# The first MLP product by Strassen's algorithm, the second product's weights in groups of four row tiles by two column tiles

## The chip, the core and the metric

The kernel runs on one core of a Trainium2 chip. The metric is device time in microseconds (us), from the runs of the compiled program. The engines named below work from queues of their own: TensorE (PE) multiplies 128x128 weight tiles by 128x320 tiles of activations into PSUM, ScalarE (ACT) and VectorE (DVE) do elementwise work, SyncE (SP) issues the loads of the weights.

## The reference, cut to what matters

The reference is one inference step of a two-layer encoder (`DEPTH = 2`) over 640 tokens: 512 of a new stream and 8 times 16 of running streams. Attention, a convolution branch and a short gated convolution are merged and projected; the part that the change touches comes after that:

```python
x = layer_norm(DN_ALPHA * x + merged @ w_mix_out, ln1_g, ln1_b)
hdn = jnp.square(jax.nn.relu(x @ w_ff1 + b_ff1))                 # 1024 -> 4096
x = layer_norm(DN_ALPHA * x + (hdn @ w_ff2 + b_ff2), ln2_g, ln2_b)   # 4096 -> 1024
```

All of it is in float32.

## The kernel before

Activations lie with features on the partitions: 8 tiles of 128 features by 640 tokens, and the tokens are worked in two halves of 320 (`HF`). Each float32 value is cut into two float32r parts (h and l), and a product of two such pairs takes three matmuls, h·h, h·l and l·h (`mm3_steps`, L357, L359 and L361). So a 1024x4096 product is 8 x 32 weight tiles x 3 matmuls x 2 halves = 1536 matmuls, and a layer's MLP has two such products.

Weights come through `Stream`. A group is 8 tiles of 128x128: one DMA of 512 KB on SP's queue into one of two `raw` buffers; ACT copies it into `wh` (L192), DVE subtracts to get `wl` (L193). Groups of the product before a norm (`mix`, `ff2`) are centred first: ACT passes over the group once for the means of its rows (L187, L188), then cuts (L189, and L190 on DVE). The cut pair lives in one of nine buffers during the MLP.

What sets the order: each engine executes a list written at build time, in which the framework's scheduler has put the instructions by their priority in the program (`tc.high_priority` moves them up). An instruction that waits holds back all that follow it on its engine.

Around the change the program does this, per layer. The output projection (`mix`) of half 0, then of half 1. The residual `r` of each half takes up the product on DVE (L333), its squares are summed (ACT L336, DVE L338), a column sum on PE (`pvn`) and a chain of twelve tiny DVE operations (L388 to L395) give the reciprocal root, PE spreads it over the partitions (`rbn`), DVE scales the eight tiles of `r` (L426), ACT and DVE cut them into `xh` and `xl` (L1043, L1044), and ACT scales `r` once more for the second residual (L1046). While half 1 goes through this, PE works on the first eight column tiles of the first MLP product for half 0 alone, 8 x 24 = 192 matmuls. Then follow the same eight for half 1, and after that chunks of four column tiles (`ff1(c)`, results `mm_ff`, through relu, square and cut on ACT and DVE as `ft`, `fq`, `hh`, `hl`) alternate with the second product of the chunk before (`ff2(c)`, results `f`, added to `r` by DVE). The last two chunks are done half by half, so that half 0's second norm lies under half 1's matmuls.

Of the kernel before, what the change touches and what calls it, by code (L numbers as in the profile page):

```python
# [19 lines left out]
P = 128  # L20
# [24 lines left out]
LOOK = 7  # L45
WARM = 12
# [22 lines left out]
def beside(i):  # L69
    """What the tensor engine does beside step i of the prompt's attention: the next heads, the absorbed queries or the side branches."""  # L70
    if i < 0:
        return "ssssss"
    if 2 <= i % 8 < 5 and i < 24:
        return "hhh"
    return "aas" if 24 <= i < 32 else "sss"


def block_groups(l):
    """The dense weights of one layer in the order of their use: groups of (name, row tile, column tile)."""
# [42 lines left out]
    for c in range(2, 8):
        ff1(c)
        if c < 7:
            ff2(c - 1)
    ff2(6)
    ff2(7)
    return g


def plan():
    out, off = [], 0
    for l in range(DEPTH):
        for g in block_groups(l):
            out.append((l, tuple(g), off))
            off += len(g) * P * P
    return out, off


def slots(g):  # L140
    """The pool of weight buffers that each group of a layer goes to."""
    n = next(i for i, q in enumerate(g) if q[0][0] == "mix")
    late = list("AAbbBBBb")
    late += [("bAAbbBBBb")[i % 9] for i in range(len(g) - n - 16)]
    return ["b"] * n + late + list("bbbbABBB")


class Stream:
    """Weights, group by group: loaded ahead and cut exactly into two float32r parts.

    Groups of the products before a norm have the mean of their rows taken off, so that
    the products have mean zero over the features."""

    def __init__(self, tc, w_ap, groups, raw_pool, part_pool, hp=400):
# [5 lines left out]
        self.held = set()  # L160

# [11 lines left out]

    def _emit(self):
        i = self.done
        self.done += 1
        _, g, off = self.groups[i]
        n, c = len(g) * P, self.slot[i]
        pp, bufs = self.pools[c]
        with self.tc.high_priority(offset=self.hp):  # L180
            raw = self.rp.tile([P, GRP * P], F32, tag="raw", name=f"raw{i}")
            self.nc.sync.dma_start(raw[:, :n], self.w[off:off + P * n].rearrange("(p n) -> p n", p=P))
            wh = pp.tile([P, GRP * P], F32R, tag="wh", name=f"wh{i}")
            wl = pp.tile([P, GRP * P], F32R, tag="wl", name=f"wl{i}")
            if g[0][0] in ("mix", "ff2"):
                nm = self.rp.tile([P, 1], F32, tag="nm", name=f"nm{i}", bufs=4)
                self.nc.scalar.activation(out=raw, in_=raw, func=AF.Copy, accum_out=nm)  # L187
                self.nc.scalar.mul(out=nm, in_=nm, mul=-1.0 / D)  # L188
                self.nc.scalar.activation(out=wh, in_=raw, func=AF.Identity, bias=nm, scale=1.0)  # L189
                self.nc.vector.scalar_tensor_tensor(out=wl, in0=raw, scalar=nm, in1=R(wh), op0=ALU.add, op1=ALU.subtract)  # L190
            else:
                self.nc.scalar.activation(out=wh[:, :n], in_=raw[:, :n], func=AF.Copy)  # L192
                self.nc.vector.tensor_tensor(out=wl[:, :n], in0=raw[:, :n], in1=R(wh[:, :n]), op=ALU.subtract)  # L193
# [3 lines left out]
    def _can(self):  # L197
# [4 lines left out]
        if c not in self.pools:  # L202
            return False
# [3 lines left out]
    def _ahead(self):  # L207
        while self._can() and self.done < self.at + (LOOK if self.groups[self.done][1][0][0] in ("mix", "ff1", "ff2") else 2):
            self._emit()
# [5 lines left out]
    def next(self, l, *keys, hold=False):  # L215
        i = self.at
        self.at += 1
        ll, g, _ = self.groups[i]
        assert ll == l and all(k in g for k in keys), (i, l, keys, ll, g)
# [10 lines left out]
        blk.i = i  # L230
        return blk
# [10 lines left out]
def trunk(tc, A, O):  # L242
# [18 lines left out]
    def open_banks(tag, **tags):  # L261
        """The PSUM banks beside psT for one phase: a pool for each name, with so many buffers."""
# [7 lines left out]
        if "op" in tags:  # L270
            # one bank for the attention's outputs, kept from phase to phase
# [15 lines left out]
    # the tensor engine's clock rises with its first products: before the data is there  # L287
# [9 lines left out]
    def split(h, lo, src, scale=None):  # L297
        """h + lo == src, 12 significant bits each."""
# [25 lines left out]
    def mm_pair(name, hs=(0, 1), ps=None):  # L324
        """One bank for each half of the tokens; the pairs of banks take turns."""
# [5 lines left out]
    def add_r(i, m, o, r, ss=None, tmp=None, tag=""):  # L331
        """r += o; ss = the sum of the squares of the tiles of r"""
# [7 lines left out]
    def center(ri, s, tag):  # L340
        """ri <- ri - its mean over the features; s is the sum of its tiles"""
# [35 lines left out]
    def rsqrt_rows(ss, starts, scale, eps, tmp, tag):  # L377
        """rs[t, c] = 1/sqrt(scale * sum_p ss[p, starts[c] + t] + eps)"""
# [850 lines left out]
```

## Time and profile before

| | |
|---|---|
| device time, median of 3 runs (lowest to highest) | 2058.18 us (2058.05 to 2060.56) |
| span of the profiled execution | 2053.8 us |
| TensorE matmul busy | 2029.3 us, 99% of the span, 13600 instructions |
| TensorE weight load busy | 1956.7 us, 95% |
| VectorE busy | 1137.9 us, 55% |
| ScalarE busy | 881.0 us, 43% |
| mean of the granted TensorE clock | 0.994 of full speed |

The span runs from the first to the last instruction of the profiled execution; the 4.4 us by which the median of the runs is longer lie around it. Busy times overlap between engines. A matmul's own duration (0.31 us) is longer than the distance from its start to the next one's start, because successive matmuls overlap; the distance is what counts. Line numbers are those of the kernel before.

### The profile page before, as it was taken

Reading aid. Unit: us, or ns where it says so; the run is one execution under the profiler, and the core shown is the slowest. Engines: PE = TensorE matmul, PEld = TensorE weight load, DVE = VectorE, ACT = ScalarE, POOL = GpSimd, SP = SyncE. Lnnn points to the kernel's source line nnn. Section 1 sums busy time; section 2 is a strip of 40 time slices with the busy share of each in tenths; the row PEclk is TensorE's granted clock in tenths of the full one; section 3 lists DMA queues with packets and bytes.
Section 4 is the critical chain, followed back from the end, with each engine's and each line's share of the span. In section 5 each row is a group of like instructions: output and inputs, shape, how many; then the busy total and the mean of one; then the engine's idle time right before and its main releaser. Section 6 shows DMA issues by size and latency. Waiting matters only on the chain.

```text
span 2053.8 us, 33262 instructions
## 1 busy us (share of the span) xinstructions
PE 2029.3 (99%) x13600; PEld 1956.7 (95%) x13600; DVE 1137.9 (55%) x2476; ACT 881.0 (43%) x1734; POOL 21.8 (1%) x39
## 2 busy tenths in 40 slices
PE   9999999999999999999999989999999999999997
PEld 9887899999999999999998878999999999999997
DVE  5754469776565333333677545697766553333335
ACT  5564222245473434445356532223354734333352
POOL 0000000000000000000010000000000000000000
PEclk9999999999999999999999999999999999999999
DMA  6113322222222222222242034222233222222111
GB/s 197 50 39 99 111 78 75 78 67 88 85 91 85 65 78 62 83 72 73 64 138 64 24 107 105 80 83 64 73 98 93 84 82 73 72 62 72 63 62 52
DMA packets 56041, 163.83 MB, mean 80 GB/s; under 512 B 10033, under 2 KB 13537, under 8 KB 55889
## 3 DMA queue, kind: packets, MB, share of 16 engines
q1 hardware_dynamic: 54016, 156.55, 24.8%
q0 software_dynamic: 1872, 5.17, 1.0%
q8 instruction: 106, 1.74, 0.4%
q14 instruction: 47, 0.38, 0.1%
HBM read 157.01 MB, written 4.69 MB: 79 GB/s over the span
## 4 chain that ended last, share of the span: by engine, by line
PE 95%; DMA 2%; ACT 1%; DVE 1%; issue 0%; SPq 0%; ACTq 0%; DVEq 0%
PE mm_ff L359 7%; PE f L359 7%; PE mm_ff L357 7%; PE mm_ff L361 7%; PE f L361 7%; PE f L357 7%; PE mm_g L357 6%; PE mm_g L359 6%; PE mm_g L361 5%; PE op L733 2%; PE mix L361 2%; PE mix L357 2%; PE mix L359 2%; DMA raw<-in_W_dram 2%; PE ol L881 1%; PE tp L720 1%
## 5 line engine op out<-in xcount | busy, mean ns | idle before, releaser
L192 ACT ACTIVATE wh<-raw 128x1024 fp32r<-128x1024 f32 (+3 forms) x186 | 183.3, 986 | 329.6 <-PE mm_g L359 201.2
L193 DVE TENSOR_TENSOR wl<-raw,wh 128x1024 fp32r<-128x1024 f32 (+3 forms) x186 | 210.7, 1133 | 193.0 <-ACT wh L192 189.8
L359 PE MATMUL f<-hl,wh 128*128 128x320 f32 x1024 | 259.3, 309 | 0.0
L357 PE MATMUL f<-hh,wh 128*128 128x320 f32 x1024 | 258.6, 308 | 0.0
L361 PE MATMUL f<-hh,wl 128*128 128x320 f32 x1024 | 258.6, 308 | 0.0
L359 PE MATMUL mm_ff<-xl,wh 128*128 128x320 f32 x1024 | 253.9, 309 | 0.0
L357 PE MATMUL mm_ff<-xh,wh 128*128 128x320 f32 x1024 | 253.6, 308 | 0.0
L361 PE MATMUL mm_ff<-xh,wl 128*128 128x320 f32 x1024 | 253.3, 308 | 0.0
L333 DVE TENSOR_TENSOR r<-r,f 128x320 f32<-128x320 f32 x256 | 116.1, 483 | 188.1 <-PE f L361 187.8
L189 ACT ACTIVATE wh<-raw,nm 128x1024 fp32r<-128x1024 f32 x80 | 90.4, 1146 | 228.2 <-PE f L359 214.7
L190 DVE SCALAR_TENSOR_TENSOR wl<-raw,nm,wh 128x1024 fp32r<-128x1024 f32 x80 | 101.5, 1283 | 155.9 <-ACT wh L189 155.8
L357 PE MATMUL mm_g<-xh,wh 128*128 128x320 f32 x768 | 181.9, 311 | 0.0
L361 PE MATMUL mm_g<-xh,wl 128*128 128x320 f32 x768 | 181.0, 309 | 0.0
L359 PE MATMUL mm_g<-xl,wh 128*128 128x320 f32 x768 | 180.5, 309 | 0.0
L361 PEld LDWEIGHTS f<-hh,wl 128*128 128x128 f32 x1024 | 177.7, 188 | 0.2
L359 PEld LDWEIGHTS f<-hl,wh 128*128 128x128 f32 x1024 | 177.7, 188 | 0.2
L357 PEld LDWEIGHTS f<-hh,wh 128*128 128x128 f32 x1024 | 177.4, 188 | 0.3
L359 PEld LDWEIGHTS mm_ff<-xl,wh 128*128 128x128 f32 x1024 | 176.5, 188 | 0.0
L357 PEld LDWEIGHTS mm_ff<-xh,wh 128*128 128x128 f32 x1024 | 176.5, 188 | 0.0
L361 PEld LDWEIGHTS mm_ff<-xh,wl 128*128 128x128 f32 x1024 | 176.4, 188 | 0.0
L187 ACT ACTIVATE raw<-raw 128x1024 f32<-128x1024 f32 x80 | 84.8, 1060 | 179.0 <-DMA raw<-in_W_dram 175.0
L977 DVE SCALAR_TENSOR_TENSOR cv<-U,vec,cv 128x320 f32<-128x320 f32 x360 | 134.0, 432 | 0.0
(330 smaller groups left out, 3859.0 us busy)
## 6 DMA issues: line engine op xcount, KB each, us to landing
raw<-in_W_dram SPq DMA_DIRECT2D x228, 512.0 KB, 3.5
kT<-in_ckvT_dram SPq DMA_DIRECT2D x16, 512.0 KB, 7.5
kM<-in_ckvM_dram SPq DMA_DIRECT2D x16, 512.0 KB, 4.4
raw<-in_W_dram SPq DMA_DIRECT2D x18, 384.0 KB, 3.1
raw<-in_W_dram SPq DMA_DIRECT2D x12, 256.0 KB, 2.7
x<-in_xT_dram SPq DMA_DIRECT2D x8, 320.0 KB, 5.9
out_y_dram<-r SPq DMA_DIRECT2D x16, 160.0 KB, 1.9
raw<-in_W_dram SPq DMA_DIRECT2D x8, 192.0 KB, 2.4
```

Source lines behind the costliest of these rows:

```text
L187: self.nc.scalar.activation(out=raw, in_=raw, func=AF.Copy, accum_out=nm)
L189: self.nc.scalar.activation(out=wh, in_=raw, func=AF.Identity, bias=nm, scale=1.0)
L190: self.nc.vector.scalar_tensor_tensor(out=wl, in0=raw, scalar=nm, in1=R(wh), op0=ALU.add, op1=ALU.subtract)
L192: self.nc.scalar.activation(out=wh[:, :n], in_=raw[:, :n], func=AF.Copy)
L193: self.nc.vector.tensor_tensor(out=wl[:, :n], in0=raw[:, :n], in1=R(wh[:, :n]), op=ALU.subtract)
L333: nc.vector.tensor_tensor(out=r[i][:, m, :], in0=r[i][:, m, :], in1=o, op=ALU.add)
L357: nc.tensor.matmul(o, wh, h[k], start=st, stop=False)
L359: nc.tensor.matmul(o, wh, lo[k], start=False, stop=False)
L361: nc.tensor.matmul(o, wl, h[k], start=False, stop=sp)
L720: nc.tensor.transpose(tp[:, kt * P:(kt + 1) * P], pb[:, kt * P:(kt + 1) * P], ident)
L733: nc.tensor.matmul(op[r0:r0 + 64, qt * P:(qt + 1) * P], vt[kt // 2][:, kt % 2, h * 64:(h + 1) * 64], pT[:, kt * P:(kt + 1) * P], start=kt ...
L977: nc.vector.scalar_tensor_tensor(out=o, in0=u, scalar=tap, in1=o, op0=ALU.mult, op1=ALU.add)
```

## The change

For the first product the activations are taken as a 2x2 matrix of blocks (lower and upper four feature tiles by half 0 and half 1: B11, B12, B21, B22) and the weights as pairs of column tiles s and s+16, so again 2x2 (a, the four lower and four upper row tiles of column s; b, those of column s+16). Each of the 16 pairs is computed in Winograd's form with 7 block products instead of 8. A block product is 4 tiles x 3 matmuls = 12, so a pair takes 84, a layer's first product 16 x 84 = 1344 matmuls instead of 1536, and the program 384 fewer.

The block products need sums of weight blocks and of activation blocks:

- Activations: T1 = B12 - B11, T2 = B22 - T1, T3 = B22 - B12, T4 = B21 - T2 are formed and cut once per layer, behind half 1's first norm (`norm_combine`, L1149 to L1173 of the kernel after). Each needs both halves, or half 1.
- Weights: per pair one set of cut buffers in up to four parts, s0 (a itself), s1 and s2 (two sums of 128x512 each on DVE into the one buffer `sm`, then a cut of 128x1024), s3 (half of b). The raw a and b of a pair stay in two buffers, `r0` (tile `rx`) and `r1` (tile `rxb`).
- Accumulators in PSUM: `C` takes B11's product, then B21's; `A` T1's, then B22's; `D` T2's; `B` T3's, then T4's. Between the two uses the content is copied or added elsewhere (`p1`, `p5`, on ACT and DVE), and the second product goes on in the same bank.
- The first four pairs (`EARLY = 4`) start with their B11 products, from plain groups that are loaded ahead; their a is loaded a second time for the sums.

The second product's groups now hold 4 row tiles by 2 column tiles (`f2(c, j)`), so a mean over a whole row is no longer in one group. The chunks 0 to 4 (`CENTERED = 5`) are multiplied uncentred and `r` is centred once after chunk 4; for chunks 5 to 7 the twelve row groups are loaded an extra time, for their means alone (kind `n`, L220 and L221), behind chunk 2; their cut then goes in pieces of 128x256 (kind `m`). The last two chunks accumulate together in PSUM for one half, then for the other, with two of the four column pairs loaded again. The means of the `mix` groups are as before. Cut buffers in the MLP are five instead of nine.

The core of the diff:

```diff
+    g.extend(("w", a1(s, 0) + a1(s, 1)) for s in range(EARLY))
+    for s, c in ff_order():
+        if c is None:
+            ff1(s)
+        else:
+            ff2(c)
+        if c == 2:
+            g.extend(("n", [("ff2", k, m) for m in range(KT)]) for cc in range(CENTERED, 8) for k in chunk(cc))
+    g.extend(f2(c, j) for j in (0, 1, 2, 3, 1, 0) for c in (6, 7))
+def ff_order():
+    o = [(0, None), (1, None)]
+    for c in range(6):
+        o += [(2 * c + 2, None), (None, c), (2 * c + 3, None)]
+    return o + [(14, None), (15, None)]
...
+            if kind == "n":
+                raw = self._load(self.rp, "raw", off, n, i)
+                j = self.nm_at[g[0][1]]
+                nc.scalar.activation(out=raw, in_=raw, func=AF.Copy, accum_out=self.nm[:, j:j + 1])
+                nc.scalar.mul(out=self.nm[:, j:j + 1], in_=self.nm[:, j:j + 1], mul=-1.0 / D)
+                return
...
+                elif kind == "s1":
+                    if len(g) > GRP:
+                        self.r0 = self._load(sp, "rx", off, n // 2, i)
+                        off += n // 2 * P
+                    self.r1 = self._load(sp, "rx", off, GRP * P, f"b{i}")
+                    self.sm = sm = sp.tile([P, GRP * P], F32, tag="sm", name=f"sm{i}", bufs=1)
+                    tt(out=sm[:, :half], in0=self.r1[:, :half], in1=self.r1[:, half:], op=ALU.add)
+                    tt(out=sm[:, half:], in0=sm[:, :half], in1=self.r0[:, :half], op=ALU.subtract)
+                    cut(sm)
+                elif kind == "s2":
+                    sm = self.sm
+                    tt(out=sm[:, :half], in0=self.r0[:, :half], in1=self.r1[:, :half], op=ALU.subtract)
+                    tt(out=sm[:, half:], in0=self.r0[:, half:], in1=sm[:, half:], op=ALU.subtract)
+                    cut(sm)
+                else:
+                    cut(self.r1[:, half:], half)
...
+            def first_of(s, blk):
+                C = bank(f"C{l}_{s}")
+                prod(C, blk.parts[0], B11)
+                p1[s] = pf.tile([P, HF], F32, tag="p1", name=f"p1_{l}_{s}", bufs=EARLY)
+                nc.scalar.activation(out=p1[s], in_=C, func=AF.Copy)
+                return C
+            def second_of(s, blk, C):
+                prod(C, blk.parts[1], B21, False, more=True)
+                hidden(s, 0, work(f"c11_{s}"), C)
...
+                A_ = bank(f"A{l}_{s}")
+                prod(A_, b1.parts[0], TX[1])
+                p5 = work(f"p5_{s}")
+                nc.scalar.activation(out=p5, in_=A_, func=AF.Copy)
...
+                prod(D_, b1.parts[1], TX[2])
+                tt(out=u2, in0=p1.pop(s), in1=D_, op=ALU.add)
+                prod(B_, b2.parts[0], TX[3])
+                tt(out=p5, in0=p5, in1=B_, op=ALU.add)
+                prod(A_, b2.parts[1], B22, False, more=True)
+                tt(out=p5, in0=p5, in1=u2, op=ALU.add)
+                hidden(s + 16, 1, p5)
+                tt(out=c12, in0=u2, in1=A_, op=ALU.add)
+                hidden(s, 1, c12)
+                prod(B_, b3.parts[0], TX[4], False, more=True)
+                tt(out=u2, in0=u2, in1=B_, op=ALU.add)
+                hidden(s + 16, 0, u2)
...
+            for s in range(EARLY + 1):
+                if s < EARLY:
+                    blk[s] = W.next(l, ("ff1", 0, s))
+                    C[s] = first_of(s, blk[s])
+                if s:
+                    second_of(s - 1, blk[s - 1], C[s - 1])
+            for s, c in ff_order():
+                if c is None:
+                    rest_of(s, s >= EARLY)
+                    if s == 0:
+                        for i, m in [(i, m) for m in range(KT) for i in range(2)]:
+                            nc.scalar.activation(out=r[i][:, m, :], in_=r[i][:, m, :], func=AF.Identity, bias=ab2[:, m:m + 1], scale=ALPHA)
+                    continue
```

Three places of the order that the change makes follow; all are in layer 0.

On PE, under half 1's first norm, the kernel before has this: the column sum `pvn` of half 1 stands among the matmuls `mm_ff` for half 0, with more of them behind it.

```order
L357 MATMUL mm_ff_2_0_6072<-xh_99,wh_5765 128x320
L382 MATMUL pvn_5925<-one_83,s_0_1_5658 128x1 [waits DVE_49,PE_49]
L382 MATMUL pvn_5925<-one_83,s_0_1_5658 128x1 x2
L359 MATMUL mm_ff_2_0_6072<-xl_101,wh_5765 128x320
L361 MATMUL mm_ff_2_0_6072<-xh_99,wl_5766 128x320
L357 MATMUL mm_ff_3_0_6103<-xh_99,wh_5789 128x320 [waits Activation_49]
```

In the kernel after, at the same place, `C_3` is the last of the four early products; `rbn` is the spreading of half 1's reciprocal root, and the first products of T1 and T2 follow at once.

```order
L446 MATMUL C_3_6128<-xh_99,wl_5781 128x320
L467 MATMUL pvn_5910<-one_83,s_0_1_5651 128x1 [waits DVE_49,PE_49]
L467 MATMUL pvn_5910<-one_83,s_0_1_5651 128x1 x2
L442 MATMUL C_3_6128<-xh_99,wh_5780 128x320
L444 MATMUL C_3_6128<-xl_101,wh_5780 128x320
L446 MATMUL C_3_6128<-xh_99,wl_5781 128x320
L486 MATMUL rbn_5931<-ident,rsyn_5915 128x128 [waits DVE_49,PE_49]
L486 MATMUL rbn_5931<-ident,rsyn_5915 128x128
L486 MATMUL rbn_5931<-ident,rsyn_5915 128x64
L442 MATMUL A_0_6192<-T1h_5904,wh_6039 128x320 [waits Activation_49]
L442 MATMUL D_0_6207<-T2h_5906,wh_6039 128x320 [waits Activation_49]
L444 MATMUL A_0_6192<-T1l_5905,wh_6039 128x320 [waits DVE_49]
```

Behind `pvn` three matmuls are left before the wait for the norm, where 122 `mm_ff` matmuls for half 0 stood before. The 24 of `A_0` and `D_0` come next, and then the B21 products of `C_0` to `C_3`, 48 matmuls, of which the first waits for ACT.

On ACT, before, the operations on the results of PE (`ft`, the relu, and `fq`, the square) stand between the cuts of the newly normed half:

```order
L1091 ACTIVATE ft0_2_0_6097<-mm_ff10_2_0_6072,vec_178 128x320 [waits PE_49]
L1092 ACTIVATE fq0_0_0_6027<-ft0_0_0_6026 128x320 [waits Activation_49]
L1043 ACTIVATE xh1_100<-r1_4537,vec_178 128x320 [waits DVE_49]
L1092 ACTIVATE fq0_1_0_6067<-ft0_1_0_6066 128x320 [waits Activation_49]
L1043 ACTIVATE xh1_100<-r1_4537,vec_178 128x320 [waits DVE_49]
```

After, the end of the list for that norm reads as follows (`t4` is cut into T4's part of `xh1`, `r0` is scaled for the second residual, `wh72` is the cut of pair 0's s2):

```order
L383 ACTIVATE xh1_100<-t4_01_6003 128x320 [waits DVE_49]
L1343 ACTIVATE r0_4537<-r0_4537,vder_180 128x320
L228 ACTIVATE wh72_6084<-sm71_6045 128x1024 [waits PE_49]
L383 ACTIVATE xh1_100<-t4_02_6007 128x320 [waits DVE_49]
L1343 ACTIVATE r0_4537<-r0_4537,vder_180 128x320
L383 ACTIVATE xh1_100<-t4_03_6011 128x320 [waits DVE_49]
L1343 ACTIVATE r0_4537<-r0_4537,vder_180 128x320
L1251 ACTIVATE p1_0_0_6037<-C0_0_6024 128x320
L1251 ACTIVATE p1_0_1_6063<-C0_1_6050 128x320
L1251 ACTIVATE p1_0_2_6103<-C0_2_6090 128x320
L1251 ACTIVATE p1_0_3_6141<-C0_3_6128 128x320
```

The four copies `p1` of PE's early products stand behind all the cuts of T1 to T4 and all sixteen scalings of `r`. From the cut of T1's first tile to the first copy there are 33 operations: 16 cuts of T tiles, 16 scalings, and `wh72`.

On SP, at the place where the row means are loaded, the last of the twelve loads (`raw107` to `raw118`) and the ones behind them are these; each of the ten later ones waits for ACT's pass over an earlier one, since there are two raw buffers. `rx119` and `rxb120` are the weights of pair 7.

```order
L206 DMA raw115_7843<-in_W_dram 128x1024 [waits DMAHW5_49,Activation_49]
L206 DMA raw116_7847<-in_W_dram 128x1024 [waits DMAHW6_49,Activation_49]
L206 DMA raw117_7851<-in_W_dram 128x1024 [waits DMAHW7_49,Activation_49]
L206 DMA raw118_7855<-in_W_dram 128x1024 [waits DMAHW0_49,Activation_49]
L206 DMA rx119_7861<-in_W_dram 128x1024 [waits DMAHW1_49]
L206 DMA rxb120_7867<-in_W_dram 128x1024 [waits DMAHW2_49]
```

The kernel before has no such loads; each of its loads is followed by that group's own use. The twelve stand on SP and their twelve passes on ACT between the cuts for chunk 2 and the cut of pair 7's a.

## Rows read from the trace of the kernel before

**Rows 1.** The page, part 1: busy us and share of each engine.
```profile
PE 2029.3 (99%) x13600; PEld 1956.7 (95%) x13600; DVE 1137.9 (55%) x2476; ACT 881.0 (43%) x1734; POOL 21.8 (1%) x39
```

**Rows 2.** The page, part 4: the chain that ended last, by engine.
```profile
PE 95%; DMA 2%; ACT 1%; DVE 1%; issue 0%; SPq 0%; ACTq 0%; DVEq 0%
```

**Rows 3.** Windows: stretch, length, busy us (instructions) per engine, clock, DMA share, GB/s.
```profile
560.00:640.00 80.00, 80.00 (x547) 79.68 (x547) 50.83 (x101) 52.67 (x107) 0.00 (x0) 1.00 0.30 93
640.00:700.00 60.00, 60.00 (x411) 60.00 (x411) 24.31 (x42) 23.02 (x44) 0.00 (x0) 1.00 0.23 71
...
1560.00:2000.00 440.00, 440.00 (x3006) 439.68 (x3005) 189.57 (x335) 202.48 (x393) 0.00 (x0) 1.00 0.24 74
```

**Rows 4.** Timeline of PE at 620 us: start, length, engine, line, operation.
```profile
619.70 0.31 PE L359 MATMUL mm_ff<-xl,wh 128*128 128x320 f32 x1
...
621.46 0.31 PE L359 MATMUL mm_ff<-xl,wh 128*128 128x320 f32 x1
```

**Rows 5.** Timeline of PE where half 1's output projection ends.
```profile
566.14 0.31 PE L361 MATMUL mix<-mgh,wl 128*128 128x320 f32 x1
566.29 0.31 PE L357 MATMUL mm_ff<-xh,wh 128*128 128x320 f32 x1
```

**Rows 6.** Timeline of DVE through half 1's first norm (in brackets: idle before).
```profile
565.13 1.22 DVE L193 TENSOR_TENSOR wl<-raw,wh 128x1024 fp32r<-128x1024 f32 x1
...
572.12 1.68 DVE L338 TENSOR_TENSOR s<-s,sqn 128x320 f32<-128x320 f32 x3
...
577.32 0.16 DVE L388 TENSOR_SCALAR rsvn<-pvn 128x3 f32<-128x3 f32 x1 [0.40 <-PE pvn L382]
...
579.49 0.16 DVE L395 SCALAR_TENSOR_TENSOR rsyn<-rstn,rsyn 128x3 f32<-128x3 f32 x1
583.76 1.46 DVE L426 SCALAR_TENSOR_TENSOR r<-r,vec,rbn 128x320 f32<-128x320 f32 x3 [4.11 <-PE rbn L401]
```

**Rows 7.** Chain of waits, 560 to 700 us: pieces on PE in that norm.
```profile
576.72 0.56 PE pvn L382 x6
583.10 0.61 PE rbn L401 x6
```

**Rows 8.** Timeline of ACT behind that norm, first and last of 27 operations.
```profile
584.34 0.56 ACT L1043 ACTIVATE xh<-r,vec 128x320 fp32r<-128x320 f32 x1 [0.89 <-DVE r L426]
...
594.83 1.00 ACT L1046 ACTIVATE r<-r,vder 128x320 f32<-128x320 f32 x2
595.74 0.46 ACT L299 ACTIVATE hh<-fq 128x320 fp32r<-128x320 f32 x1
```

**Rows 9.** Timeline of ACT around 566 us: weight cuts that wait for their load.
```profile
563.59 1.06 ACT L192 ACTIVATE wh<-raw 128x1024 fp32r<-128x1024 f32 x1 [1.24 <-DMA raw<-in_W_dram]
...
566.83 1.06 ACT L192 ACTIVATE wh<-raw 128x1024 fp32r<-128x1024 f32 x1 [1.11 <-DMA raw<-in_W_dram]
567.80 0.82 ACT L336 ACTIVATE sqn<-r 128x320 f32<-128x320 f32 x2
569.89 1.06 ACT L192 ACTIVATE wh<-raw 128x1024 fp32r<-128x1024 f32 x1 [1.27 <-DMA raw<-in_W_dram]
```

**Rows 10.** Groups by line, 580 to 1018 us, on DVE: count, busy us, mean ns.
```profile
L193 DVE TENSOR_TENSOR wl<-raw,wh 128x1024 fp32r<-128x1024 f32 x28 | 34.2, 1222 | 48.0 <-ACT wh L192 48.0
```

**Rows 11.** The same on ACT: the pass for the means, and the relu.
```profile
L187 ACT ACTIVATE raw<-raw 128x1024 f32<-128x1024 f32 x30 | 31.8, 1059 | 77.8 <-DMA raw<-in_W_dram 77.8
L1091 ACT ACTIVATE ft<-mm_ff,vec 128x320 f32<-128x320 f32 x64 | 30.4, 515 | 2.7 <-PE mm_ff L361 2.7
```

**Rows 12.** Timeline of PE where it stood idle longest.
```profile
1219.30 0.64 PE L357 MATMUL mm_gc<-xh,wh 128*128 128x320 f32 x1 [5.05 <-ACT gcs L510]
```

**Rows 13.** Windows around that idle time (columns as in rows 3).
```profile
1215.00:1220.00 5.00, 0.70 (x3) 0.71 (x4) 2.92 (x5) 3.90 (x6) 0.00 (x0) 0.83 0.41 127
1220.00:1225.00 5.00, 5.00 (x21) 4.88 (x21) 2.80 (x7) 1.60 (x4) 0.00 (x0) 0.50 0.29 109
1225.00:1230.00 5.00, 5.00 (x35) 4.38 (x34) 0.42 (x1) 0.44 (x1) 0.00 (x0) 0.98 0.03 7
```

More of the change, by code (lines that the diff above doesn't have):

```diff
@@ L45 @@
 LOOK = 7
+EARLY = 4
+CENTERED = 5
+HB = (8, 6)
 WARM = 12
@@ L133, in plan @@
     for l in range(DEPTH):
-        for g in block_groups(l):
-            out.append((l, tuple(g), off))
-            off += len(g) * P * P
+        for kind, g in block_groups(l):
+            out.append((l, kind, tuple(g), off))
+            off += len(g) * P * P if g[0][0] != "set" else 0
     return out, off
 def slots(g):
[L142 to L145, printed above, removed]
+    n = next(i for i, (_, q) in enumerate(g) if q[0][0] == "mix")
+    out, j = ["b"] * n + list("AbbBBBBb"), 0
+    for kind, _ in g[n + 8:]:
+        out.append(None if kind == "n" else "bAbbb"[j % 5])
+        j += kind != "n"
+    return out
 class Stream:
@@ L172, in _free, with _load @@
         return i <= self.at - 3 and i not in self.held
+    def _load(self, pool, tag, off, n, i):
+        raw = pool.tile([P, GRP * P], F32, tag=tag, name=f"{tag}{i}")
+        self.nc.sync.dma_start(raw[:, :n], self.w[off:off + P * n].rearrange("(p n) -> p n", p=P))
+        return raw
     def _emit(self):
@@ L176, in _emit @@
         self.done += 1
-        _, g, off = self.groups[i]
+        _, kind, g, off = self.groups[i]
         n, c = len(g) * P, self.slot[i]
-        pp, bufs = self.pools[c]
+        nc, half = self.nc, GRP * P // 2
         with self.tc.high_priority(offset=self.hp):
-            raw = self.rp.tile([P, GRP * P], F32, tag="raw", name=f"raw{i}")
-            self.nc.sync.dma_start(raw[:, :n], self.w[off:off + P * n].rearrange("(p n) -> p n", p=P))
+            if kind == "n":
[4 more added lines that the diff above has]
+                return
+            pp, bufs = self.pools[c]
@@ L201, in _can @@
         c = self.slot[i]
-        if c not in self.pools:
+        if c is None:
+            return self.nm is not None
+        if c not in self.pools or self.groups[i][1][0] == "s" and self.set_pool is None:
             return False
@@ L207, in _ahead @@
     def _ahead(self):
-        while self._can() and self.done < self.at + (LOOK if self.groups[self.done][1][0][0] in ("mix", "ff1", "ff2") else 2):
+        while self._can() and self.done < self.at + (2 if self.groups[self.done][1] == "w" and self.groups[self.done][2][0][0] not in ("ff1", "ff2") else LOOK):
             self._emit()
@@ L215, in next @@
     def next(self, l, *keys, hold=False):
+        while self.groups[self.at][1] == "n":
+            if self.done <= self.at:
+                self.prefetch()
+            self.at += 1
         i = self.at
         self.at += 1
-        ll, g, _ = self.groups[i]
-        assert ll == l and all(k in g for k in keys), (i, l, keys, ll, g)
+        ll, kind, g, _ = self.groups[i]
+        assert ll == l and all(k in g or k == kind for k in keys), (i, l, keys, ll, kind, g)
         if hold:
@@ L230, in next @@
         blk.i = i
+        blk.parts = [[(wh[:, j * P:(j + 1) * P], wl[:, j * P:(j + 1) * P]) for j in range(4 * h, 4 * h + 4)] for h in range(2)]
         return blk
@@ L349, in add_s, with mm3_steps @@
             nc.vector.tensor_tensor(out=s, in0=ri[:, 0, :] if m == 1 else s, in1=ri[:, m, :], op=ALU.add)
-    def mm3_steps(outs, blocks, xs, first=True, last=True):
+    def mm3_steps(outs, blocks, xs, first=True, last=True, more=False):
         n = len(blocks)
@@ new lines, in trunk @@
+                if i == 0:
+                    ln_scale(r[0], ss, KT, D, V("l1g", 0, KT), pl, f"n1{l}0")
+                    for j in range(KT):
+                        cut_x(0, j, V("l1b", j))
+            lm.close()
+            xT = xt_stk.enter_context(pool(f"xT{l}"))
+            T_own = {j: [xT.tile([P, 4, HF], F32R, name=f"T{j}{n}{l}") for n in "hl"] for j in (1, 2, 3)}
+            TX = {j: [[t[:, k, :] for k in range(4)] for t in T_own[j]] for j in T_own}
+            TX[4] = [[x[1][:, k, :] for k in range(4)] for x in (xh, xl)]
```

275 lines of the change are left out of this document (183 added, 92 removed).

## The prediction

> **What bounds the kernel now.** I read the page's shares first: PE's matmuls are busy 99% of the span, DVE 55%, ACT 43% [rows 1]. The chain that ended last is PE for 95% [rows 2], so nearly every microsecond off PE's list is one off the span, and every one in which PE waits is added. The windows say where this holds: in the MLP PE is busy 80.00 of 80.00, 60.00 of 60.00 and 440.00 of 440.00 us, at full clock, with DVE and ACT at some 40% in the steady part [rows 3]. So the two MLPs have no wait at all to lose, and spare time on both helpers. The timeline gives the price of a matmul: 12 steps between the first and last row take 1.76 us, 0.147 each [rows 4]; products for half 0 alone start at the same distance, 0.15 [rows 5], so block products for one half are no dearer.
>
> **The gain.** 384 matmuls x 0.147 = 56.3 us, 28.2 per layer. Everything else about the change is a question of whether PE waits. The sum is made against the profiled span of 2053.8 us; the median of the runs is 4.4 us above it, and no edit touches what lies around the span, so I add the difference to 2058.2. The whole gain without a wait would be 2001.9.
>
> **The first norm of half 1 (once per layer).** Zero is PE's first matmul behind `mix` (566.29 before [rows 5]). Before, 192 matmuls for half 0 alone, 28.2 us, stood over this norm. After, only 48 do, 7.1 us, and all that comes next needs half 1 or ACT. Step by step:
> - PE comes to `pvn` after 45 matmuls, at 6.6. The sum of squares was ready 7.5 after zero in the kernel before (573.80 [rows 6]), with three weight cuts of DVE among it that the new order has ahead; I take it as ready in time. From `pvn` to the first tiny operation 0.6 [rows 6, 7]: 7.2.
> - The root chain took 577.32 to 579.65, 2.3 us [rows 6]. In the new order a weight cut (1.22 [rows 10]) and two 512-wide sums (no row shows one; half of that row each, 1.2 together) stand within it: 2.3 + 2.4 gives 11.9.
> - `rbn` to the first scaled tile 0.66 (583.10 to 583.76 [rows 6, 7]): 12.6. Eight scalings at 1.46/3 = 0.49: 16.5. The first difference and T1's first cut can start at about 17.2.
> - The B21 products of C_0 to C_3 need only data that is there, but the bank of C_0 must be copied first, and that copy is the 34th operation on ACT from there. 27 operations of this kind took 584.34 to 595.74, 0.42 each [rows 8]: 32 x 0.42 + 1.06 for the weight cut [rows 9] + 0.42 for the copy = 14.9. So C_0 goes on at 32.1.
> PE has had 72 matmuls by then (10.6 us) and some 1.2 us of `pvn` and `rbn`: it is idle for 32.1 - 11.8 = **20.3 us**. Bounds: 17.9 if the three DVE operations within the root chain cost nothing; 23.4 if each ACT operation takes the relu's whole 0.515 [rows 11].
>
> **The clock.** After 5.05 us of idle PE [rows 12] the granted clock is 0.50, the lower level of 1.2 GHz, in the next 5 us, with 21 matmuls in place of 34, and 0.98 after that [rows 13]. That is 13 x 0.147 = 1.9 us lost, and with the first two or three slow ones before 1220 **2.3 us**. The idle stretches in this norm are of that length, so I charge it once per layer; the 24 matmuls of A_0 and D_0 are paced by their operands anyhow. The Trainium skill (TensorE: Matmul & The Clock Gate, section on HAM oscillation) has a matmul engine that waits between short bursts fall to the lower clock in every burst; by that each longer wait below would pay the 2.3 us too. That is the third rival's clock.
>
> **Twelve extra loads (once per layer).** They share two raw buffers. From the end of a cut's use (565.13 + 1.22 = 566.35 [rows 6]) to the next ACT operation on that buffer (569.89 [rows 9]) are 3.54 us. So a buffer's round is 1.06 for the pass [rows 11] + 3.54 = 4.6. Zero here is the first matmul of the second product's chunk 2. The first pass can begin when chunk 2's third group is cut and its buffer loaded again, about 4.9; the second buffer follows about 7.7, behind ACT's evictions of pair 6. Its sixth pass ends at 7.7 + 5 x 4.6 + 1.06 = 31.8. Pair 7's a is loaded by then, its cut on ACT ends at 32.9, on DVE at 34.1. PE is there after 204 matmuls, 29.9: first 3.0, then for `wl` some 0.9 more, and in the pairs behind, for a copy and for pair 8's a, 1.5. With half a chance of the clock's 2.3: **6.5 us**. Bounds: 2 if the first pass comes a round earlier; 14 if loads come at the 3.15 us of the cuts that waited for a load (563.59, 566.83, 569.89 [rows 9]): last pass over at 40.6, cut at 41.7, which is 11.8 late, and the same 1.5.
>
> **Pairs next to each other.** Pairs 0, 1, 2 and 13, 14, 15 stand three in a row with no second product between. (Where two stand together, as 5 and 6, the second's loads run under the chunk before, and I count nothing.) The buffer of b is free after its last cut; load 3.54, two sums 1.2, cuts 1.06 and 1.22 make 7.0 us until the next A can go on. PE has 36 matmuls, 5.3 us, in that time: some 1.7 per junction, and where the copies queue on ACT more. Four junctions, one of them covered by the early products: **6 us** per layer with the start of the last chunks. Bounds 2 and 10.
>
> **What costs nothing.** DVE gets 447 instructions more and ACT 127; in a layer's MLP of some 420 us DVE's busy time goes from about 190 us to about 300 (16 pairs x four sums and three or four cuts, T1 to T4, evictions), still below PE, so hidden on average; where it isn't, it is in the terms above. Centring once after chunk 4: 16 sums and 16 subtractions on DVE, with a chunk of 192 matmuls (28 us) over it: 0 to 3 us, I take **1**. The 35 loads more in the program: DMA's share is 0.22 to 0.30 in the MLP [rows 3], so not bandwidth but the order on SP counts, and that is in the twelve loads. The end of the program stays as it is.
>
> **Sum.** Waits per layer 20.3 + 2.3 + 6.5 + 6 + 1 = 36.1, twice 72.2; less 56.3: +15.9, so 2058.2 + 15.9 = **2074** us. The change breaks even at 28.2 us of waits per layer. With the lower bounds together (17.9 + 2.3 + 2 + 2 + 0 = 24.2 per layer) 2050; with the upper ones (23.4 + 2.3 + 14 + 10 + 3 = 52.7) 2107.
>
> **Rivals.**
> - *The norm is the only place.* The loads of the means begin early enough, since SP and the raw buffers are free for long stretches, and the junctions hide under the pairs' other work. Then the waits are 22.6 per layer, below the 28.2: 2058.2 + 45.2 - 56.3 = 2047. For it: helpers at 40% [rows 3]. Against it: in the order the passes stand behind pair 6's evictions. It decides as soon as pair 7 is on time and the junctions cost under 5 us together.
> - *Nearly all of it is gained.* The norm's wait is half of what I count, because ACT's scalings and cuts run in waits and the copies come at 20 rather than 32: 10 + 2.3 per layer and no other wait, 2027; without any, 2002. Against it: the copy's place in ACT's list, behind 33 operations at 0.42, none of which can start before 12.6.
> - *The loads at the measured spacing, with the clock falling at each long wait:* 20.3 + 2.3 + 14 + 2.3 + 8 + 2 = 48.9 per layer, 2100. For it: 3.15 us is what the trace shows between loaded cuts [rows 9]. Against it: those cuts also waited for DVE, which the passes don't need.
> - *The change does not shorten PE's list as it says,* because single-half products are dearer. Excluded as far as rows go: the same distance [rows 4, 5].
>
> **How the numbers follow.** 0.42 for the forecast (waits of 32 to 42 per layer, 2066 to 2086), 0.20 for the slow loads (2086 to 2110), 0.16 for the norm alone (2036 to 2054), 0.12 for more of the gain (2000 to 2036), and 0.10 for between (2054 to 2066). Less than 0.2%, 4 us, can't be told from no change by a measurement of this kernel; of the last case a bit more than half lies there. So faster 0.29, same 0.08, slower 0.63. The likeliest case's own range is 2064 to 2088; the range that leaves a tenth out on each side is 2028 to 2104.
>
> **What would show it.** In the profile after: PE's matmuls 384 fewer; windows of the MLP with PE below full only at four kinds of place. The waits of PE should list `rbn` on DVE, A_0 and D_0 on ACT and DVE, and above all C_0's second part on ACT, with about 20 us together per layer and a clock of 0.5 to 0.8 around it. Next, C_7 and its `wl` behind ACT, some 4 us; then A_2, A_14, A_15. I am wrong in the first place if C_0's second part starts much before 32 us from the end of `mix`, in the second if C_7 does not wait or waits over 8 us; and wrong about the sign if the waits per layer sum to less than 28 us.

## The result and the profile after

The changed kernel takes 2091.82 us (median of 4 runs, 2091.26 to 2092.82), the kernel before 2058.64 beside it (4 runs, 2058.05 to 2060.56). The ratio is 1.016, with a 95% interval of 1.0146 to 1.0175: 33.2 us slower, where 15.9 were forecast. The profiled execution has a span of 2089.2 us and a mean granted clock of 0.974 (0.994 before). The experiments ran on three chips, on which the kernel before took 2054.2 to 2055.0 (medians), so they are compared by their ratio to it; 0.001 of ratio is 2.06 us.

The page's busy times after, to be set against [rows 1]:

```profile
PE 2000.0 (96%) x13216; PEld 1919.3 (92%) x13216; DVE 1366.4 (65%) x2958; ACT 951.5 (46%) x1870; POOL 21.8 (1%) x39
```

and the chain that ended last, against [rows 2]:

```profile
PE 85%; DMA 6%; DVE 4%; ACT 4%; issue 1%; SPq 0%; ACTq 0%; DVEq 0%
```

The 384 matmuls are gone, and PE's share of the chain fell from 95% to 85%: for a tenth more of the span the chain goes through loads and the helpers. PE's waits say where (total us, times, longest):

```profile
PE C L442 <- ACT wh L228: 15.9, 2, 8.6
PE rbn L486 <- DVE rsyn L480: 11.3, 3, 4.5
PE C L442 <- ACT p L1251: 11.0, 4, 5.2
PE A L442 <- ACT T1h L383: 9.6, 2, 4.8
PE mm_gc L442 <- ACT gcs L596: 8.6, 2, 5.0
PE D L442 <- ACT T2h L383: 5.2, 2, 2.6
PE A L442 <- ACT wh L228: 5.2, 2, 2.9
PE f L442 <- ACT wh L246: 3.0, 1, 3.0
PE A L444 <- DVE T1l L384: 2.2, 2, 1.1
```

Most have the count 2: one per layer. The first is C_7 behind the twelve loads; `rbn`, `C` on `p`, `A` on `T1h` and `D` on `T2h` belong to the norm of half 1; `A` on `wh` is A_2. (`mm_gc` lies in the mixer ahead of the MLP and waited before as well [rows 12].)

The length of a layer's MLP, from the first matmul behind `mix` to the last `f`, went from 453.9 in both layers to 470.0 (569.4 to 1039.4) and 473.4. With the gain of 28.2 put back, waits and slow matmuls cost 44.3 and 47.7 per layer, against a forecast of 36.1.

The norm of half 1 in layer 0, on PE (start, length, operation, in brackets idle before), where [rows 5 and 7] stood:

```profile
569.36 0.31 PE L442 MATMUL C<-xh,wh 128*128 128x320 f32 x1
575.96 0.72 PE L467 MATMUL pvn<-one,s 128*128 128x1 f32 x6
581.50 1.51 PE L486 MATMUL rbn<-ident,rsyn 128*128 128x128 f32 x6 [4.27 <-DVE rsyn L480]
587.81 0.63 PE L442 MATMUL A<-T1h,wh 128*128 128x320 f32 x1 [4.80 <-ACT T1h L383]
591.06 0.64 PE L442 MATMUL D<-T2h,wh 128*128 128x320 f32 x1 [2.62 <-ACT T2h L383]
593.89 0.63 PE L444 MATMUL A<-T1l,wh 128*128 128x320 f32 x1 [1.09 <-DVE T1l L384]
603.56 0.64 PE L442 MATMUL C<-xh,wh 128*128 128x320 f32 x1 [4.72 <-ACT p L1251]
```

The last row is C_0's second part, 34.2 us after the first. Its releaser is at the end of ACT's list, as in the order shown before:

```profile
587.30 0.45 ACT L383 ACTIVATE T1h<-t 128x320 fp32r<-128x320 f32 x1
...
597.61 0.47 ACT L383 ACTIVATE T3h<-t 128x320 fp32r<-128x320 f32 x1 [0.69 <-DVE t L1167]
...
602.64 0.55 ACT L1343 ACTIVATE r<-r,vder 128x320 f32<-128x320 f32 x1
603.09 1.38 ACT L1251 ACTIVATE p<-C 128x320 f32<-128x320 f32 x4
```

The windows (columns as in [rows 3]) show the clock around both places, and an undisturbed stretch:

```profile
580.00:585.00 5.00, 1.51 (x6) 1.35 (x6) 3.08 (x12) 0.00 (x0) 0.00 (x0) 0.60 0.39 105
585.00:590.00 5.00, 0.63 (x1) 0.29 (x1) 5.00 (x12) 4.54 (x11) 0.00 (x0) 0.50 0.00 0
...
600.00:605.00 5.00, 1.44 (x5) 1.44 (x6) 3.47 (x7) 4.46 (x11) 0.00 (x0) 0.65 0.00 0
605.00:610.00 5.00, 5.00 (x25) 5.00 (x25) 0.49 (x1) 2.09 (x5) 0.00 (x0) 0.67 0.00 0
...
630.00:635.00 5.00, 4.13 (x18) 3.87 (x19) 5.00 (x8) 5.00 (x9) 0.00 (x0) 0.72 0.07 29
...
680.00:720.00 40.00, 40.00 (x275) 40.00 (x274) 25.47 (x43) 15.90 (x26) 0.00 (x0) 1.00 0.30 106
...
770.00:775.00 5.00, 1.99 (x14) 1.73 (x12) 0.00 (x0) 2.12 (x5) 0.00 (x0) 1.00 0.62 170
775.00:780.00 5.00, 0.00 (x0) 0.00 (x0) 0.00 (x0) 2.50 (x7) 0.00 (x0) 0.56 0.64 260
780.00:785.00 5.00, 3.93 (x12) 3.13 (x12) 3.22 (x5) 0.62 (x2) 0.00 (x0) 0.50 0.00 1
```

In the steady part all is as forecast (275 matmuls in 40 us, 0.145 each). Where PE stood, it goes on at 0.50, the lower level of 1.2 GHz, or, behind A_2's wait of 2.92 us at 630.46, at a window's mean of 0.72: the first steps there are some 0.15 us long as before, from 632.29 on a dozen of 0.27 follow. Before C_7 PE does nothing for a whole window, DVE neither, and ACT works half the time: only the loads are busy. ACT's passes for the means, and the cut of pair 7's a behind them:

```profile
746.50 1.04 ACT L220 ACTIVATE raw<-raw 128x1024 f32<-128x1024 f32 x1
749.87 1.06 ACT L220 ACTIVATE raw<-raw 128x1024 f32<-128x1024 f32 x1 [0.78 <-DMA raw<-in_W_dram]
...
774.30 1.06 ACT L220 ACTIVATE raw<-raw 128x1024 f32<-128x1024 f32 x1 [1.50 <-DMA raw<-in_W_dram]
778.12 1.06 ACT L220 ACTIVATE raw<-raw 128x1024 f32<-128x1024 f32 x1 [2.43 <-DMA raw<-in_W_dram]
779.47 1.06 ACT L228 ACTIVATE wh<-rx 128x1024 fp32r<-128x1024 f32 x1
```

and pieces of the chain of waits there (start, length):

```profile
746.41 3.43 DMA raw<-in_W_dram
...
755.94 4.40 DMA raw<-in_W_dram
761.53 4.44 DMA raw<-in_W_dram
767.17 4.23 DMA raw<-in_W_dram
772.59 5.50 DMA raw<-in_W_dram
```

The passes begin with a load of 3.43, near the 3.54 of the forecast; later the loads on the chain take 4.2 to 5.5. For comparison, the window of the kernel before in which most of the 3.54 lies has less traffic:

```profile
565.00:570.00 5.00, 5.00 (x36) 5.00 (x36) 4.90 (x10) 2.62 (x6) 0.00 (x0) 1.00 0.52 185
```

### The profile page after: what moved, and what is told of

Read it like the earlier page. It is cut to its first block, busy times and chain, and to the rows that moved or that the text cites. A ratio compares the mean times of both kernels' runs of the same rounds, so it can differ in the third digit from the quotient of the medians.

```text
span 2089.2 us, 33051 instructions
## 1 busy us (share of the span) xinstructions
PE 2000.0 (96%) x13216; PEld 1919.3 (92%) x13216; DVE 1366.4 (65%) x2958; ACT 951.5 (46%) x1870; POOL 21.8 (1%) x39
## 4 chain that ended last, share of the span: by engine, by line
PE 85%; DMA 6%; DVE 4%; ACT 4%; issue 1%; SPq 0%; ACTq 0%; DVEq 0%
PE f L442 6%; PE f L446 6%; PE f L444 6%; PE mm_g L442 5%; PE mm_g L444 5%; PE mm_g L446 5%; DMA raw<-in_W_dram 4%; PE op L819 2%; PE mix L446 2%; PE mix L442 2%; PE mix L444 2%; PE C L442 2%; PE C L446 2%; PE C L444 2%; PE A L446 2%; PE A L442 2%
## 5 line engine op out<-in xcount | busy, mean ns | idle before, releaser
L417 DVE TENSOR_TENSOR r<-r,f 128x320 f32<-128x320 f32 x192 | 85.2, 482 | 98.5 <-PE f L446 98.2
L442 PEld LDWEIGHTS mm_g<-xh,wh 128*128 128x128 f32 x768 | 129.7, 188 | 1.5 <-issue 0.3
L446 PEld LDWEIGHTS mm_g<-xh,wl 128*128 128x128 f32 x768 | 129.6, 188 | 0.2
L444 PEld LDWEIGHTS mm_g<-xl,wh 128*128 128x128 f32 x768 | 129.4, 188 | 0.3
L228 ACT ACTIVATE wh<-sm 128x1024 fp32r<-128x1024 f32 x64 | 67.6, 1056 | 106.2 <-PE f L444 57.4
L442 PE MATMUL C<-xh,wh 128*128 128x320 f32 x256 | 84.4, 330 | 26.8 <-ACT wh L228 15.9
L229 DVE TENSOR_TENSOR wl<-sm,wh 128x1024 fp32r<-128x1024 f32 x64 | 78.2, 1222 | 34.5 <-PE C L446 19.7
L446 PE MATMUL C<-xh,wl 128*128 128x320 f32 x256 | 83.3, 326 | 0.7 <-DVE wl L229 0.7
L444 PE MATMUL C<-xl,wh 128*128 128x320 f32 x256 | 83.1, 325 | 0.0
L442 PE MATMUL mix<-mgh,wh 128*128 128x320 f32 x256 | 78.9, 310 | 0.0
```

What stands on the lines that cost most here:

```text
L228: nc.scalar.activation(out=wh[:, :n], in_=src, func=AF.Copy)
L229: nc.vector.tensor_tensor(out=wl[:, :n], in0=src, in1=R(wh[:, :n]), op=ALU.subtract)
L417: nc.vector.tensor_tensor(out=r[i][:, m, :], in0=r[i][:, m, :], in1=o, op=ALU.add)
L442: nc.tensor.matmul(o, wh, h[k], start=st, stop=False, skip_group_check=more)
L444: nc.tensor.matmul(o, wh, lo[k], start=False, stop=False, skip_group_check=more)
L446: nc.tensor.matmul(o, wl, h[k], start=False, stop=sp, skip_group_check=more)
```

## The experiments

**1. The early copies out of their place.** The theory: the wait of C_0's second part is the place of the four `p1` copies at the end of ACT's list.

```diff
-p1[s] = pf.tile([P, HF], F32, tag="p1", name=f"p1_{l}_{s}", bufs=EARLY)
-nc.scalar.activation(out=p1[s], in_=C, func=AF.Copy)
+p1[s] = xT.tile([P, HF], F32, tag="p1", name=f"p1_{l}_{s}", bufs=EARLY)
+with tc.high_priority(offset=100):
+    nc.scalar.activation(out=p1[s], in_=C, func=AF.Copy)
```

> The four p1 copies get memory that the norm's temporaries do not hold (a tag in the pool of T1 to T3) and a higher priority, so that they stand in ACT's list ahead of the cuts of T1 to T4; nothing else changes. Theory 1 (the copies' place in ACT's list costs): the 48 matmuls of the B21 products (7.0 us) move under the norm's chain and the wait of 4.7 us behind D_0 goes; some of it comes back at B_0. 7 to 10 us less per layer, so 2072 to 2078 us against 2091.8. Rival (the norm's chain on DVE is what PE waits for, and the moved matmuls only move the wait to B_0): under 4 us less per layer, 2084 or more.

Measured: 2090.21 us (four runs from 2082.6 to 2097.2), ratio 1.0172 (1.0142 to 1.0202), no gain against 1.016. The copies did move up, and C's wait on `p` fell to 1.1 us, but a longer wait took its place. PE in layer 0, and, on DVE, the sum of weights that stands behind this wait:

```profile
608.30 0.64 PE L442 MATMUL A<-T1h,wh 128*128 128x320 f32 x1 [24.93 <-ACT wh L228]
```

```profile
605.07 0.68 DVE L260 TENSOR_TENSOR sm<-rxb 128x512 f32<-128x512 f32 x1
```

In the changed kernel this sum stood at 574.34, ahead of the norm's tail; here it comes behind it. In the built program's addresses the copies' new place (5120 bytes per partition) had pushed `sm` 96 bytes into the space of one of the norm's temporaries, and in the order that was built pair 0's weights are formed only once T1 to T4 are cut. The edit therefore tested something else than the theory. Experiment 5 mends it.

**2. The twelve loads spread.** One load for the means behind each second-product group of chunks 1 to 3, in place of twelve behind chunk 2.

```diff
-if c == 2:
-    g.extend(("n", [("ff2", k, m) for m in range(KT)]) for cc in range(CENTERED, 8) for k in chunk(cc))
+for j in range(4):
+    g.append(f2(c, j))
+    if 1 <= c < 4:
+        g.append(("n", [("ff2", chunk(c + 4)[j], m) for m in range(KT)]))
```

> The twelve loads for the row means, with their passes on ACT, go one behind each of the groups of the second product's chunks 1 to 3 instead of all behind chunk 2. Same loads, same passes, same bytes. Theory (the burst holds up pair 7's weights on SP and ACT): the waits of C_7 (8.6, 0.4 and 0.5 us in layer 0) and 26 matmuls at half clock (3.1 us) go, some 12.5 us per layer, to 2067 us; C_7 waits for nothing in the trace. Rival (their volume costs, wherever they stand): new waits at other places, less than 5 us per layer won, 2082 or more.

Measured: 2058.12 us, ratio 1.002 (1.001 to 1.0031). That is 0.014 below the changed kernel, 29 us or 14.4 per layer, a little more than the 12.5 expected; the MLPs take 454.0 and 460.5, 16.0 and 12.9 less. C_7's wait is gone, and the same window is full at full clock:

```profile
775.00:780.00 5.00, 5.00 (x36) 5.00 (x35) 3.70 (x7) 3.69 (x6) 0.00 (x0) 1.00 0.00 0
```

**3. Both edits.**

> Both edits. If the two places are independent the gains add: 2091.8 - 18 - 25 = about 2049 us, 10 below the kernel before. If a wait only moves from one place to the other, it stays above 2058.6.

Measured: 2063.05, ratio 1.0041 (1.0027 to 1.0055), no better than the spread loads alone, and not the 2049 expected: experiment 1's new wait of 24.9 us is here too.

**4. The clock at C_7.** 44 matmuls whose result nobody reads, just ahead of C_7, so that PE does not stand while it waits.

```diff
+if s == 7:
+    wu7 = psT.tile([P, 512], F32, tag="t", name=f"wu7{l}")
+    for i in range(44):
+        nc.tensor.matmul(wu7[:, :HF], hd[22, 0][0][:, :P], hd[22, 0][0], start=True, stop=True)
```

> The kernel after with 44 matmuls more per layer (128x320, on data that is there, into a bank that nobody reads) right ahead of C_7's first matmul. They take 6.5 us of the 8.6 us in which PE stands idle there; the loads are as before. Theory (the lower clock after each long wait is a cost of its own): the clock stays at 1.00 there and the 26 matmuls behind at 0.267 us go at 0.147: 3.1 us less per layer, 2085.5 us. Rival (those matmuls wait for their operands anyway, so the clock costs nothing): no change, 2092.

Measured: 2090.45, ratio 1.0176 (1.0161 to 1.0191), no gain; the MLPs take 470.2 and 474.5. PE at that place, and the windows:

```profile
771.52 6.62 PE L1343 MATMUL wu<-hh 128*128 128x320 f32 x44
779.99 0.41 PE L442 MATMUL C<-xh,wh 128*128 128x320 f32 x1 [1.85 <-ACT wh L228]
781.24 0.51 PE L446 MATMUL C<-xh,wl 128*128 128x320 f32 x1 [0.70 <-DVE wl L229]
```

```profile
775.00:780.00 5.00, 3.15 (x23) 2.89 (x21) 0.04 (x1) 3.19 (x7) 0.00 (x0) 1.00 0.71 287
780.00:785.00 5.00, 4.06 (x14) 3.28 (x14) 3.82 (x6) 1.06 (x1) 0.00 (x0) 0.66 0.01 3
```

The edit did only a part of what it was meant to do. The clock stays at 1.00 while the extra matmuls run. But PE still waits 1.85 and 0.70 us for pair 7's weights, and behind these waits nine steps are 0.27 us long again (781.55 to 783.69); the mean of the window is 0.66, where it was 0.50. PE's list changed as well: 12 of C's matmuls stand ahead of A_7 here and 24 in the changed kernel, so the distance from C_7 to A_7 can't be compared. The distance from the end of the second product's chunk to the end of the next 132 matmuls, of the same kinds in both kernels, can: 31.6 us here, 33.1 in the changed kernel. That is 1.6 less in layer 0, of the 3.1 expected. A_2's wait, which lies ahead of this place and which the edit does not touch, was 4.3 instead of 2.9 in this execution, and hides it in the layer's length. Twice 1.6 us are 0.0015 of ratio, as much as either side of each interval, so the experiment is inconclusive: what the clock's price behind this wait is in the kernel's time stays open.

**5. The early copies with room.** Experiment 1, with the norm's temporaries in nine buffers instead of ten, so that `sm` lies apart from them.

```diff
-return tmp.tile([P, HF], F32, tag="tt", name=f"{n}{l}{k}", bufs=10)
+return tmp.tile([P, HF], F32, tag="tt", name=f"{n}{l}{k}", bufs=9)
```

> As e1, with one more edit: the norm's temporaries get 9 buffers instead of 10, 1280 bytes per partition, so that the space of pair 0's weight sum does not reach into theirs, as it did by 96 bytes in e1. In the built order pair 0's and pair 1's weights are then cut under the norm's chain, and the copies p1 stay early. Theory (e1's gain was there and was eaten by pair 0's weights, which waited for the norm's memory, 24.9 us at A_0): the wait at A_0 falls from 24.9 to about 5, B_0 starts some 32 us behind mix instead of 43, 11 to 16 us less per layer than the kernel after, 2060 to 2070 us beside its 2091.8. Rival (the norm's chain sets the end of this stretch whatever the order): 2085 or more.

Measured: 2073.09, ratio 1.0096 (1.008 to 1.0111), 0.0064 or 13 us below the changed kernel, a little under 7 per layer; the MLPs of the profiled execution, the fastest of four, take 459.7 and 465.9 (10.3 and 7.5 less). A_0's wait of 24.9 for its weights is gone. The expected 11 to 16 per layer were not reached, and the waits tell why:

```profile
PE C L442 <- ACT wh L228: 14.6, 2, 8.2
PE A L442 <- ACT T1h L383: 11.4, 2, 5.9
PE B L442 <- ACT c L1243: 9.6, 2, 5.0
PE D L442 <- ACT T2h L383: 7.0, 2, 3.5
```

C's 48 matmuls now fill the wait for `rbn` (its row in the norm and C's on `p` are gone there), but `B_0` waits up to 5.0 for the eviction of C (`c`), which stands in ACT's list where the copies stood. ACT's list behind the norm is no shorter (18.4 us from T1's first cut to `c`, where it was 15.8 to the copies); another instruction now waits for its end.

**6. Both, with room** (2 and 5).

> e5's edits and e2's spread loads. If the two are independent, e2's gain of 32 us (2058.1 against 2090.5 in the same call) and e5's of 22 to 32 add: 2030 to 2040 us, faster than the kernel before (2054.6 to 2058.6) by 0.8 to 1.3%. Rival: 2054 or more, if what waits behind is late by the same chain.

Measured: 2047.4 us (2046.44 to 2050.39), ratio 0.9967 (0.9955 to 0.998). This beats both kernels, the one before by 0.3% and the changed one by 1.9%. The MLPs take 448.2 and 455.7. The two edits now add up: the spread loads are worth 0.0129 against experiment 5, and 0.014 alone. The 2030 to 2040 expected were missed because they took 22 to 32 us for the early copies, and these measured 13.

**7 and 8. Without the loads of the means,** with experiment 5's edit and with the change alone.

```diff
-if c == 2:
-    g.extend(("n", [("ff2", k, m) for m in range(KT)]) for cc in range(CENTERED, 8) for k in chunk(cc))
...
+nc.vector.memset(W.nm, 0.0)
```

> e5's edits, and the twelve loads for the row means per layer are left out with their passes; the means are set to zero instead (the centring of chunks 5 to 7 is left out of the computation). Theory (spread, the loads cost nothing): within 3 us of e6. Rival (their volume on DMA and ACT still costs something when spread): e6 is more than 5 us slower than this.

> The kernel after without the twelve loads per layer and their passes (the means are set to zero, so the centring of chunks 5 to 7 is left out of the computation); the norm as it was. It gives the whole price of the loads in a row: as e2, within 3 us (2058), if spreading hides all of them; 5 to 10 us below e2 if it hides only the wait at C_7.

Measured: 2049.11, ratio 0.9978 (0.9968 to 0.9987), and 2060.03, ratio 1.003 (1.0019 to 1.004). The kernels with spread loads have 0.9967 and 1.002: the loads cost nothing when spread, so all of the 27 to 29 us is the price of having twelve in a row.

**9. The scalings of r on GpSimd.** Experiment 6, with ACT's sixteen scalings behind the norm given to another engine.

```diff
-nc.scalar.activation(out=r[i][:, m, :], in_=r[i][:, m, :], func=AF.Identity, bias=ab2[:, m:m + 1], scale=ALPHA)
+nc.gpsimd.tensor_scalar(out=r[i][:, m, :], in0=r[i][:, m, :], scalar1=ALPHA, scalar2=ab2[:, m:m + 1], op0=ALU.mult, op1=ALU.add)
```

> This is e6_room_spread with the sixteen scalings of r for the second residual behind the norm (one 128x320 operation each, 0.42 us apart on ACT) given to GpSimd instead. What it asks: is the rest of the wait behind the first norm set by ACT's list, as the prediction's norm step has it? If so, B_0, which in e6 waits 5.0 us for ACT's eviction of c11, comes earlier by up to 16 x 0.42 = 6.7 us of ACT's list, as far as the wait goes: its row falls from 9.6 us in two waits to under 3, PE is 4 to 5 us earlier per layer, and the time is 2037 to 2042 against 2047 for e6 (0.992 to 0.994 of the kernel before). The rival: DVE, not ACT, is what bounds that stretch (it forms and cuts T1 to T4 there; its window after the norm was 5.00 of 5.00 us in the changed kernel), or GpSimd slows DVE down: then the waits on T1h and T2h stay or grow, and the time is 2045 to 2055.

Measured: 2050.97, ratio 0.9984 (0.9975 to 0.9993), not faster than 0.9967; the rival's range and its waits hold. In layer 0 and 1 together PE's waits on `T2h` and on C's eviction grew from 7.0 to 8.5 and from 9.6 to 10.5. The same operation on DVE, first in experiment 6, then in this one:

```profile
589.32 1.47 DVE L1137 SCALAR_TENSOR_TENSOR xl<-r,vec,xh 128x320 fp32r<-128x320 f32 x3
```

```profile
589.06 1.94 DVE L1137 SCALAR_TENSOR_TENSOR xl<-r,vec,xh 128x320 fp32r<-128x320 f32 x3
```

and what GpSimd does meanwhile:

```profile
587.07 5.06 POOL L1345 TENSOR_SCALAR r<-r,vder 128x320 f32<-128x320 f32 x4 [356.47 <-ACT xh L1136]
596.50 13.49 POOL L1345 TENSOR_SCALAR r<-r,vder 128x320 f32<-128x320 f32 x12 [4.37 <-DVE t L1168]
```

These operations of DVE are longer by a third while GpSimd works; in its pause, from 592.1 to 596.5, two cuts of T1 take 0.88 us where they took 0.89. ACT, with a shorter list, waits for DVE instead (in layer 0 `T3h` on `t` 3.5 us in three waits, 0.2 in experiment 6). The Trainium skill (GPSIMD Engine Reference, section Architecture) says that GpSimd reads and writes through ports that it shares with VectorE. The 1.47 and 1.94 us agree with that. In experiment 6 DVE has no idle time from 582.9 to 606.2, so a shorter list on ACT had little to win. But since this edit also slowed DVE down, it does not show how much of the wait ACT's list alone would give back.

## Why the prediction was right in sign and wrong in size

- **The gain was right.** 13216 matmuls, and 0.145 us each in the steady part; no helper fell behind there.
- **The norm of half 1 was right in mechanism and nearly in size.** `rbn` began 12.1 us after zero (forecast 11.9), T1's first cut at 17.9 (17.2), C_0's second part at 34.2 (32.1). Of these 2.1, 0.9 are `rbn`, which took 1.51 us instead of 0.61 [rows 7]: PE had stood for 4.27 before it, and the window shows 0.60. Another 1.3 are waits of ACT's list for DVE's `t` (0.69 the longest). That A_0 and D_0 went at half speed costs nothing here, since PE waited 4.72 behind them. Of the 34.2 us, 11.8 are work: 22.4. Behind it, 30 matmuls between 603.56 and 610 where 44 fit cost 2.0 more. That is 24.4, with 22.6 forecast for wait and clock together. Experiment 5 adds that the copies' place in ACT's list, on which the forecast laid the whole wait, gives back only some 7 of the 24 when it is mended; the rest moves to other waits of the same chain on DVE and ACT.
- **The step that failed is "So a buffer's round is 1.06 for the pass [rows 11] + 3.54 = 4.6."**, in the part on the twelve extra loads. The times around it held. Its zero, the first matmul of chunk 2's second product, is 741.91; the second buffer's first pass came 8.0 later (forecast 7.7), and PE stood at C_7 after 30.1 (29.9). But from 749.87 to 778.12 five rounds take 28.25, 5.65 each instead of 4.6 (5.29 in layer 1). Five times the difference is 5.3: pair 7's cut ended 38.6 after zero instead of 32.9, and C_7 waited 8.59 instead of 3.0 (7.3 in layer 1). The 8.59 are over the 8 us at which the prediction called itself wrong here. The 3.54 came from a stretch in which a load overlapped the other buffer's by only 0.5 us (566.35 to 566.83), and the DMA share was 0.52. In the burst a load, as the one from 755.94 to 760.34, has the other buffer's beside it until 757.65 and again from 758.8; the share is 0.62 to 0.64, and a load takes 4.2 to 4.4. The last one, 5.50, has pair 7's two loads behind it on the queue. That loads in flight together make each other longer is read from these rows; no run changes that alone.
- **What the burst cost.** With 0.4 for `wl`, 0.5 for the copy, and 3.1 for 26 matmuls at half the clock (0.12 more each), layer 0 has 12.6 in the rows, against a term of 6.5. Experiments 2 and 8 put the whole at 13.4 to 14.4 per layer. So the error of this term is 6 to 8 per layer, 12 to 16 of the 17 us by which the forecast fell short. The other errors cancel in part: the norm 1.8 too low, junctions and centring 1 too high each, and in layer 0 some 2 us that no row names.
- **The clock was charged at half there**, with 2.3 us x 1/2. The window behind C_7 shows 0.50, and the price by the rows is 3.1; this is 2 of the 6. The Trainium skill (TensorE: Matmul & The Clock Gate, section on HAM oscillation) has an engine that waits between bursts start each burst at the lower clock. The rows at C_7 and in the norm show that too; at A_2 the burst starts at the full clock's distance and the clock falls 1.8 us later. Experiment 4 could not settle what the price is in the kernel's time.
- **Pairs next to each other** were one junction, not three: A_2 waits 2.9 us, with 0.4 for `wl` and the clock behind it some 5 in layer 0 (18 matmuls in 4.13 busy us of a window, which fit into 2.7 at full clock), where 6 were forecast for several junctions. Pairs 13 to 15 have no wait.
- **Centring** shows no wait of PE (1 forecast). The counts under "What costs nothing" were a little low (DVE has 482 instructions more and ACT 136, and 40 loads were added), which no term of the sum uses. A wait of 3.0 for `f` in layer 1's last chunks was folded into the junctions' term.
- **The sign** was right because the norm's 24 us are most of the 28.2 at which the change breaks even; any second wait of more than 4 us makes it slower, and there were two. The third rival, slow loads with the clock falling at each wait, was the nearer one: it had 2100, with loads at 3.15 where the passes came 2.8 apart.

The rival "the norm is the only place" is nearly what experiment 2 builds (A_2's wait stays): it forecast 2047, 0.995 of the kernel before, and the kernel without the burst has 1.002. So the burst alone does not explain the loss of the whole gain; the norm, A_2 and small waits take 28 us in layer 0 by themselves (454.0 against 453.9) and 35 in layer 1.

## What to carry to other kernels

A duration of a load taken where loads come one at a time is not the one of a burst: when several loads are put in a row on one queue, price the round with both buffers in flight, or spread them between the loads that the work needs anyway, which here made them free. When an algorithm saves multiplications by needing both halves of the data, look at what the saved or moved work was covering; here it covered a norm. And a buffer that is put elsewhere can change which others share space, and by that the order: read the waits of the run before the verdict on the idea.

## What was not expected of the hardware

The loads of 512 KB on the chain took 3.4 to 3.7 us at the start of the burst and 4.2 to 4.4, once 5.5, later in it, with another in flight. An idle time of 2.9 us at A_2 was followed by a clock of 0.72 in its window, as longer ones were by 0.50; in experiment 4 the same followed waits of 1.85 and 0.70 us, with 0.66. And GpSimd, at some 1.17 us for an operation that takes ACT 0.55, made three DVE operations beside it take 1.94 us instead of 1.47.
